# Seven inputs of a Winograd-style convolution loaded as fp32 through nine rotating slots, one casting load left

## The chip, the cores and the metric

The kernel runs on one core of one Trainium2 chip. The metric is the device time of one execution in microseconds (us). A ratio is the mean time of one kernel's fast runs over that of the kernel before in the same rounds, so it is not quite the ratio of the medians quoted beside it.

In the profile PE is TensorE (matmuls), PEld its weight loads, DVE VectorE, ACT ScalarE, POOL GpSimd and SP SyncE, whose queue starts most transfers. A "casting load" is a transfer from HBM that reads fp32 and writes fp16 into SBUF; only GpSimd issues those here, on the software queue q0. All other transfers of the program are on the hardware queue q1; q8 and q14 fetch instructions. A transfer is cut into packets for the 16 DMA engines, and it has landed when all its engines have reported.

## The reference

```python
batch, c_in, h, w, c_out = 16, 64, 64, 64, 128
x_pad = np.pad(x, ((0, 0), (0, 0), (1, 1), (1, 1)), mode='constant')
for b in range(batch):
    for co in range(c_out):
        for ci in range(c_in):
            for kh in range(3):
                for kw in range(3):
                    output[b, co] += weight[co, ci, kh, kw] * x_pad[b, ci, kh:kh+h, kw:kw+w]
```

The input is 16.8 MB of fp32, the output 33.6 MB. Both must cross HBM once.

## The kernel before

Two images form a pair: 64 channels each, 128 partitions together, eight pairs in all. Rows are taken two at a time, so that two output rows share one product `U` of the sum of two input rows (`ss`). TensorE takes fp16, so each fp32 input needs a cast. Pairs 0 to 4 come as fp32 and are cast by ScalarE in quarters; pairs 5 to 7 come through casting loads.

```python
NH = 5
def next_slot(shape, name):                     # 16 KB per partition each
    slot[0] += 1
    return big.tile(shape, F32, tag=f"slot{(slot[0] - 1) % 8}", name=name)

def load(p):                                    # fp32, hardware queue
    xf[p] = next_slot([128, H, W], "xf")
    for lo, hi in cuts if p == 0 else [(0, H)]: # input 0 in four pieces
        keep(nc.sync.dma_start(xf[p][:, lo:hi, :], x_rows[128 * p : 128 * p + 128, lo:hi, :]))

def cast(p, n):
    if p not in xs:
        xs[p] = xpool.tile([128, H, W], F16, tag="xs", name="xs")
    lo, hi = cuts[n]
    keep(nc.scalar.copy(xs[p][:, lo:hi, :], xf[p][:, lo:hi, :]))

def outs(p):
    ots[p] = [next_slot([128, H // 2, 2, W], "ot") for _ in range(2)]

def load_cast(p):                               # fp32 to fp16 on the way
    xs[p] = xpool.tile([128, H, W], F16, tag="xc", name="xc")
    keep(nc.gpsimd.dma_start(xs[p], x_rows[128 * p : 128 * p + 128, :, :]))
# ... weights, sums of pair 0 ...
for p in range(NP):
    # ... GpSimd adds the row pairs of input p + 1; at p == 0 the casting loads are issued
    for blk in range(4):                        # 8 row pairs each
        U = group([(G1, None)])                 # matmuls on ss
        # ScalarE copies U out of PSUM, then runs casts[p][blk]
        A = group([(G21, 1), (G0, -1)])         # VectorE: even rows = A + U
        Bt = group([(G01, 0), (G2, 2)])         # VectorE: odd rows = Bt + U
        # ... after the last block: two stores of 2 MB (the last pair: two halves each)
```

## Time and profile before

| what | before |
|---|---|
| time, median of 4 runs (beside the changed kernel) | 127.97 us |
| span of the profiled run | 126.2 us |
| TensorE busy | 106.4 us, 84% |
| hardware queue q1 / casting loads q0, share of 16 engines | 84.0% / 12.1% |
| ScalarE casts | 20 |

The span is the profiled execution from first to last instruction. "Share of 16 engines" is the time that a queue's packets took, divided by 16 times the span. The lines themselves are in the prediction, with how to read them.

### The profile page before, as it was taken

The numbers are of one execution on the slowest core, as the hardware profiler recorded it, in microseconds if no ns is written. First come the engines' busy times: TensorE is split into PE (matmuls) and PEld (weight loads), VectorE is DVE, ScalarE is ACT, GpSimd is POOL, SyncE is SP. The second block draws the span as 40 slices with busy tenths as digits, with TensorE's granted clock in tenths as the row PEclk, the third lists the DMA queues.
The fourth block names the chain that finished last, engine by engine and source line by source line (L and its number), as shares of the span: only waits on it lengthen the run. The fifth ranks groups of instructions, "written<-read, shape, count | busy, mean of one in ns | idle before, by whom it ended". The sixth has DMA issues, their size and how long they took to land.

```text
span 126.2 us, 2428 instructions
## 1 busy us (share of the span) xinstructions
PE 106.4 (84%) x978; PEld 53.6 (42%) x978; DVE 84.4 (67%) x135; ACT 55.9 (44%) x88; POOL 33.8 (27%) x23
## 2 busy tenths in 40 slices
PE   0479999999999999999999999999999999950000
PEld 0334545554454545454545454455545554520000
DVE  0186777877777777777877787777877787770000
ACT  4183789996969694333333333333333333300000
POOL 2000399959129258004800390000000000000000
PEclk9999999999999999999999999999999999996555
DMA  4999999999999999999999999999999999999970
GB/s 121 298 434 431 426 426 436 343 317 317 288 332 332 312 309 306 369 447 447 410 415 421 436 452 426 415 415 426 452 436 415 421 415 462 423 395 434 423 301 10
DMA packets 4330, 47.62 MB, mean 377 GB/s; under 512 B 480, under 2 KB 480, under 8 KB 1120
## 3 DMA queue, kind: packets, MB, share of 16 engines
q1 hardware_dynamic: 3888, 44.34, 84.0%
q0 software_dynamic: 432, 3.15, 12.1%
q8 instruction: 7, 0.11, 0.3%
q14 instruction: 3, 0.02, 0.0%
HBM read 17.07 MB, written 33.55 MB: 401 GB/s over the span
## 4 chain that ended last, share of the span: by engine, by line
PE 82%; DMA 4%; DVE 2%; issue 1%; DVEq 0%; SPq 0%
PE acc L170 82%; DMA xf<-in_x_dram 4%; DVE ot L190 1%; DVE ss L95 1%; DVE ot L193 0%; DVEq L227 0%; SPq L51 0%; DVEq L190 0%
## 5 line engine op out<-in xcount | busy, mean ns | idle before, releaser
L170 PEld LDWEIGHTS <-Wt 64*128 64x128 f16 x960 | 52.5, 96 | 53.8 <-issue 4.1
L184 ACT COPY ut<-acc 128x512 f32<-128x512 f32 x64 | 34.4, 591 | 49.8 <-issue 45.2
L170 PE MATMUL acc<-xs,Wt 64*128 64x504 f16 (+2 forms) x480 | 56.5, 383 | 0.0
L190 DVE TENSOR_TENSOR ot<-acc,ut 128x512 f32<-128x512 f32 x64 | 41.3, 687 | 22.0 <-PE acc L170 19.6
L193 DVE TENSOR_TENSOR ot<-acc,ut 128x512 f32<-128x512 f32 x64 | 41.2, 685 | 0.6 <-PE acc L170 0.6
L170 PE MATMUL acc<-xc,Wt 64*128 64x504 f16 (+3 forms) x288 | 32.7, 373 | 0.0
L170 PE MATMUL acc<-ss,Wt 64*128 64x504 f16 (+1 forms) x192 | 27.0, 384 | 1.5 <-DVE ss L95 1.5
L95 POOL TENSOR_TENSOR ss<-xf 128x1024 f16<-128x1024 f32 x8 | 18.8, 2378 | 20.0 <-DMA xf<-in_x_dram 15.0
L68 ACT CAST xs<-xf 128x1024 f16<-128x1024 f32 (+2 forms) x20 | 20.4, 1060 | 0.9 <-DMA xf<-in_x_dram 0.9
L95 POOL TENSOR_TENSOR ss<-xc 128x1024 f16<-128x1024 f16 x6 | 12.6, 2125 | 21.0 <-issue 21.0
L113 PE MATMUL wp<-ident,w 128*64 128x128 f16 x18 | 1.3, 328 | 4.2 <-DVE w L85 4.2
L95 DVE TENSOR_TENSOR ss<-xf 128x512 f16<-128x512 f32 x4 | 2.8, 690 | 2.8 <-DMA xf<-in_x_dram 2.8
L85 DVE CAST w<-w_raw 128x576 f16<-128x576 f32 x1 | 0.5, 460 | 3.7 <-DMA w_raw<-in_weight_dram 3.7
L113 PEld LDWEIGHTS <-w 128*64 128x64 f16 x18 | 1.1, 209 | 4.2 <-DVE w L85 4.2
L77 POOL DMA_DIRECT2D xc<-in_x_dram x3 | 1.8, 599 | 0.0
L115 ACT CAST Wt<-wp 128x384 f16<-128x384 f32 x1 | 0.5, 480 | 2.8 <-PE wp L113 2.8
L115 ACT ACT_TABLE_LOAD x1 | 1.3, 1283 | 0.7 <-PEq L216 0.7
L120 ACT CAST Wt<-wp 128x384 f16<-128x384 f32 x1 | 0.5, 481 | 0.5 <-DVE Wt L118 0.5
L117 DVE TENSOR_TENSOR Wt<-wp,Wt 128x384 f16<-128x384 f32 x1 | 0.6, 551 | 0.0
L118 DVE TENSOR_TENSOR Wt<-wp,Wt 128x384 f16<-128x384 f32 x1 | 0.5, 549 | 0.0
L121 ACT CAST Wt<-wp 128x384 f16<-128x384 f32 x1 | 0.5, 487 | 0.0
masks.py:199 POOL TENSOR_SCALAR_AFFINE_SELECT ident<-ident 128x128 f16<-128x128 f16 x1 | 0.3, 293 | 0.1
(5 smaller groups left out, 0.6 us busy)
## 6 DMA issues: line engine op xcount, KB each, us to landing
out_dram<-ot SPq DMA_DIRECT2D x14, 2048.0 KB, 20.4
xf<-in_x_dram SPq DMA_DIRECT2D x4, 2048.0 KB, 19.6
out_dram<-ot SPq DMA_DIRECT2D x4, 1024.0 KB, 11.4
xc<-in_x_dram POOLq DMA_DIRECT2D x3, 1024.0 KB, 24.2
xf<-in_x_dram SPq DMA_DIRECT2D x2, 512.0 KB, 6.2
xf<-in_x_dram SPq DMA_DIRECT2D x1, 576.0 KB, 5.0
xf<-in_x_dram SPq DMA_DIRECT2D x1, 448.0 KB, 7.2
w_raw<-in_weight_dram SPq DMA_DIRECT2D x1, 288.0 KB, 2.9
```

What stands on the lines that cost most here:

```text
L68: keep(nc.scalar.copy(xs[p][:, lo:hi, :], xf[p][:, lo:hi, :]))
L77: keep(nc.gpsimd.dma_start(xs[p], x_rows[128 * p : 128 * p + 128, :, :]))
L85: keep(nc.vector.tensor_copy(w16, w_raw))
L95: eng.tensor_add(ss[p][:, lo : lo + n, :], v[:, lo : lo + n, 0, :], v[:, lo : lo + n, 1, :])
L113: nc.tensor.matmul(wp[q : q + 64, k * CO : k * CO + CO], w16[:, t::9], ident)
L115: keep(nc.scalar.copy(wrow(G1), wps[1]))
L117: keep(nc.vector.tensor_sub(wrow(G21), wps[2], wrow(G1)))
L118: keep(nc.vector.tensor_sub(wrow(G01), wps[0], wrow(G1)))
L170: nc.tensor.matmul(tiles[b2][:, lo - j0 : hi - j0, c_lo:c_hi], Wt[p0 : p0 + 64, wi, kw, :], rhs, start=i == 0, stop=i == n - 1,)
L184: keep(nc.scalar.copy(ut, U[b2]))
L190: nc.vector.tensor_add(ots[p][b2][:, j0 : j0 + RB, 0, :], A[b2], us[b2])
L193: nc.vector.tensor_add(ots[p][b2][:, j0 : j0 + RB, 1, :], Bt[b2], us[b2])
```

## The change

The intent is to take two of the three casting loads off GpSimd's queue. Seven fp32 inputs need more slots (nine) and a deeper ring of fp16 inputs (four). ScalarE, which gets eight more casts, is spared two of them by GpSimd. One buffer of row sums is given up, and the row sums of pairs 3 and 4 are now taken from the fp16 copies. (Changed lines only, without their context.)

```diff
-    xpool = ctx.enter_context(tc.tile_pool(name="xpool", bufs=3))
+    xpool = ctx.enter_context(tc.tile_pool(name="xpool", bufs=1))
-    spool = ctx.enter_context(tc.tile_pool(name="spool", bufs=3))
+    spool = ctx.enter_context(tc.tile_pool(name="spool", bufs=2))
-    NH = 5
+    NH = 7
-        return big.tile(shape, F32, tag=f"slot{(slot[0] - 1) % 8}", name=name)
+        return big.tile(shape, F32, tag=f"slot{(slot[0] - 1) % 9}", name=name)
+    by_pool = [(3, 3), (5, 3)]
-            xs[p] = xpool.tile([128, H, W], F16, tag="xs", name="xs")
+            xs[p] = xpool.tile([128, H, W], F16, tag=f"xs{p % 4}", name="xs")
-        keep(nc.scalar.copy(xs[p][:, lo:hi, :], xf[p][:, lo:hi, :]))
+        copy = nc.gpsimd.tensor_copy if (p, n) in by_pool else nc.scalar.copy
+        keep(copy(xs[p][:, lo:hi, :], xf[p][:, lo:hi, :]))
-    casts[1] = [[(2, 0), (2, 1)], [(2, 2)], [(2, 3), (3, 0)], [(3, 1)]]
-    casts[2] = [[(3, 2), (3, 3)], [(4, 0)], [(4, 1), (4, 2)], [(4, 3)]]
+    casts[1] = [[(2, 0), (2, 1)], [(2, 2), (2, 3)], [(3, 0), (3, 1)], [(3, 2)]]
+    casts[2] = [[(4, 0), (4, 1)], [(4, 2), (4, 3)], [(5, 0), (5, 1)], [(5, 2)]]
+    casts[3] = [[(6, n)] for n in range(4)]
-                sums(nc.gpsimd, p + 1, xf[p + 1] if p + 1 < NH else xs[p + 1], lo, 16)
+                sums(nc.gpsimd, p + 1, xf[p + 1] if p < 2 else xs[p + 1], lo, 16)
+            if p == 1 or p == 2:
+                cast(2 * p + 1, 3)
```

## The prediction

> **What bounds the kernel now.** I began with the page: the busy shares, the row of forty slices and the DMA queues.
>
> ```profile
> PE 106.4 (84%) x978; PEld 53.6 (42%) x978; DVE 84.4 (67%) x135; ACT 55.9 (44%) x88; POOL 33.8 (27%) x23
> ...
> PE   0479999999999999999999999999999999950000
> ...
> DMA  4999999999999999999999999999999999999970
> GB/s 121 298 434 431 426 426 436 343 317 317 288 332 332 312 309 306 369 447 447 410 415 421 436 452 426 415 415 426 452 436 415 421 415 462 423 395 434 423 301 10
> ...
> q1 hardware_dynamic: 3888, 44.34, 84.0%
> q0 software_dynamic: 432, 3.15, 12.1%
> ```
>
> The reader is to see two full rows, not one. TensorE is full from slice 4 to slice 35 and then has nothing to do; the DMA row is full from slice 2 to slice 39, so it begins earlier and ends later. q0 is the three casting loads, q1 all else.
>
> Next the chain of work that ended last, then busy time by stretch.
>
> ```profile
> 1.18 5.03 DMA xf<-in_x_dram
> ...
> 6.97 103.93 PE acc L170 x948
> ...
> 112.85 0.60 DVE ot L193
> ```
>
> The program's own last arithmetic is done at 113.5 us of 126.2. The chain looks like TensorE (82%), but it stops there; the other 12.7 us are the landing of outputs and the end of the program, which it does not attribute. (The last line is a piece of the page's chain in order of time: start, length, what.)
>
> ```profile
> 9.00:21.50 12.50, 12.50 (x106) 6.03 (x104) 8.95 (x15) 9.11 (x14) 6.76 (x6) 1.00 1.02 435
> 21.50:54.50 33.00, 33.00 (x313) 16.67 (x311) 26.08 (x43) 23.45 (x34) 17.95 (x8) 1.00 1.02 330
> 54.50:111.00 56.50, 56.50 (x532) 28.51 (x530) 44.00 (x72) 19.36 (x36) 8.42 (x4) 1.00 1.01 428
> ...
> 114.00:120.00 6.00, 0.00 (x0) 0.00 (x0) 0.00 (x0) 0.00 (x0) 0.00 (x0) 0.54 1.00 423
> 120.00:126.20 6.20, 0.00 (x0) 0.00 (x0) 0.00 (x0) 0.00 (x0) 0.00 (x0) 0.50 0.36 153
> ```
>
> The last two columns are DMA share and GB/s. The share is 1.00 to 1.02 in every stretch from 9 to 120 us. The apparent dip to 330 GB/s in the middle is counting: bytes are those written, and a casting load reads twice what it writes. In those 33 us 330 x 33 = 10.9 MB were written; adding the other half that the casting loads read, 3.15 MB, gives 14.04 MB, or 425 GB/s. So the DMA engines are the bound, TensorE close behind. How close: the last output transfers are issued at 114.5 us (the end of SyncE's row in the timeline). From there 5.5 us x 423 + 6.2 us x 153 = 3.3 MB still move, of which those last transfers are 2.1 MB. The other 1.2 MB are a backlog of 2.8 us. A compute end later by less than that, minus the start delay of a transfer, costs nothing; one earlier gains nothing.
>
> **What the Trainium skill says.** "DMA: Bandwidth & Descriptors", section "Bandwidth", gives 435 GB/s as the ceiling of the ports into SBUF and 425 measured for a 16 MB transfer; the trace agrees, with 435, 425 and 428. The same page, section "SWDGE vs HWDGE vs iDMA", says that a cast during a DMA must be issued from GpSimd, and that software and hardware queues feed the same 16 engines, which take turns between them. The trace agrees: in the casting stretch the two share one total that stays at 425. So taking a load off the one queue and putting it on the other makes no new capacity. "GPSIMD Engine Reference", section 4.1, calls one-input GpSimd work roughly line-rate, and two-input work about half the speed of VectorE. The first page's "Specifications" put the start delay of a hardware-queue transfer at about 0.6 us, which no view here separates; with it the backlog is an estimated 2.2 us. For two inputs on GpSimd this trace has 2.37 us for 1024 columns; a GpSimd cast it does not show.
>
> **The change, part by part.**
>
> *Loads.* Two casting loads leave, two fp32 loads of 2 MB come. In DMA time: q0 has 12.1% for three, that is 4.03% or 5.09 us each; q1 has 84.0% for 44.34 MB, 1.894% per MB, or 3.97% and 5.01 us for a 2.10 MB load. Saved: 2 x 0.08 = 0.16 us. The rates say the same: 425 against 428 over 33 us is 0.23 us for three loads, 0.15 us for two. If pure loading keeps the 435 of the first stretch, two more loads save another 0.16 us. Sum: 0.15 to 0.3 us off the bound. Total bytes from and to HBM do not change.
>
> *Order.* Seven loads now stand ahead of the outputs in the one hardware queue, so the first output (ready at 23.2 us) begins to move at about 45 us instead of 34 to 37. By 45 us 17.07 MB must have been read: 1.2 us start, about 3.3 us lost in the first 6 us, 17.07 MB at 425 = 40.2 us, sum 44.7. The outputs, 33.55 MB at 428, take 78.4 us: 123.1, where the transfers end now too. The queue does not run dry between: pair k's output is ready at about 23 + 12.8k us, and gets its turn at 44.7 + 9.8k; for pair 6 that is 100 against 103.5.
>
> *Slots.* With nine slots, pair 1 writes into the slots of inputs 0 and 1, pair 3 into 4 and 5, pair 4 into input 6 and the first output. That output is sent by about 50 us and its slot is wanted at 74. No slot looks late.
>
> *ScalarE.* Eight casts more, minus two given to GpSimd, against the 20 of now: 26. At 1.06 us (mean of the row of casts) plus 0.59 us per copy, a block with two casts and two copies takes 2.12 + 1.18 = 3.3 us by means; a block on TensorE lasts 12.8 / 4 = 3.2. Copies overlap in the timeline (two take 1.07), so it is 3.2. Pair 0 already has three blocks like this:
>
> ```profile
> 16.75 1.07 ACT L184 COPY ut<-acc 128x512 f32<-128x512 f32 x2 [0.43 <-ACT xs L68]
> 17.71 2.11 ACT L68 CAST xs<-xf 128x1152 f16<-128x1152 f32 x2
> 19.99 1.07 ACT L184 COPY ut<-acc 128x512 f32<-128x512 f32 x2 [0.17 <-ACT xs L68]
> ```
>
> There 0.17 to 0.43 us remain idle, so it just fits, and each fourth block of pairs 1 and 2 has one cast and lets it catch up.
>
> *Arrival.* Inputs 2 and 3 should land as now, input 3 at 27.4 us. Inputs 4, 5 and 6, with one casting load beside them, land at about 35, 40 and 45 us. ScalarE wants them after the copies of pair 2's first block (36.9 us now), of its third (43.3) and of pair 3's first (49.7). The margin is 2 to 5 us.
>
> *GpSimd.* Two casts of 896 columns, which I estimate at 1.2 us each: the two-input add reads 2048 elements in 2.37 us, 1.16 ns each, times 896, and a little. The next sums wait for a free buffer, since there are two instead of three. Pair 3's sums cannot start before TensorE has used those of pair 1, about 32 us, and need 4.2 us, against the 48 us at which they are wanted. This is off the path.
>
> Sum: 127.95 - 0.25 = 127.7 us.
>
> **The rivals.**
>
> *Casting loads are dearer than they look* (descriptor work on GpSimd, stalls). Then two fewer would save more. Against it: their packets' share per byte read is within 2% of the others', and the DMA share never falls below full while they run. The most it could give is the 2.8 us of backlog, where TensorE's end takes over: about 125.3 us.
>
> *A new wait on ScalarE or GpSimd.* If a load comes after ScalarE asks for it, the copies behind it in program order wait, PSUM stays full and TensorE stops. For it: input 4's margin is under 2 us and the blocks are full. Against it: 2.2 to 2.8 us of backlog swallow the first stall. A stall of 3 us would make 128.5 to 130; one at every block with two casts, up to 1 us each over the nine blocks of pairs 0 to 2 that have two casts, 127.7 + 9 - 2 = 135.
>
> *The hidden transfer.* The load's place in time is all that changes, and both queues are behind one full bound: the time stays at 127.9. My main case is this one with the small saving on top.
>
> **Range and chances.** The saving is 0.15 to 0.3 us and the runs before spread 0.3 us. I give 127.0 to 128.6, with a little more room above, for a stall that the backlog does not wholly swallow. Over 2% faster means under 125.4, all that the backlog allows: 0.02. Slower than 130.5 needs a repeated stall: 0.04. Within 2%: 0.94.
>
> **What would show each step.** Right: the DMA row full to slice 38; about 1.05 MB on q0 with some 4% share; 430 GB/s or so in place of 310 to 340 for most of 21 to 54 us; outputs taking 25 us or more to land in the middle; the chain still 104 us of TensorE, its last VectorE add at 113.5 within half a microsecond. Wrong: TensorE below 9 in slices 8 to 16, with casts waiting on the input's DMA; a DMA row with a slice below 9 after slice 20, which would mean that the outputs ran dry; or a last add well after 115 us.

## The result, and the profile after

The changed kernel takes 127.95 us (median of 4 runs, 127.78 to 128.12) beside 127.97 us for the kernel before; the ratio is 1.000, with a 95% interval of 0.998 to 1.0021. Run again later in five rounds (the twelfth run below) it took 127.94 beside 127.91, ratio 0.9994. No change shows. The predicted 127.7 us would be a ratio of 0.998: it lies at the edge of the first interval and inside that of the twelfth run (0.9961 to 1.0027), so the times alone do not exclude a saving of 0.25 us.

From the page of the changed kernel, the DMA row in forty slices, the rate, and the two queues:

```profile
DMA  4999999999999999999999999999999999999960
GB/s 122 304 431 443 427 426 426 348 320 317 393 432 427 429 429 427 421 432 421 437 437 416 442 416 432 437 421 421 432 421 437 437 416 442 413 406 437 429 265 13
...
q1 hardware_dynamic: 4176, 48.53, 91.8%
q0 software_dynamic: 144, 1.05, 4.0%
```

The stretch below 350 GB/s in the middle has shrunk from nine slices to three, because only one casting load is left, but the DMA row above it is as full as it was. The two queues took 96.1% before and take 95.8% now: work went from one to the other.

Busy time by stretch of the changed kernel, at the cuts shown of the kernel before; the last two columns are DMA share and GB/s:

```profile
9.00:21.50 12.50, 12.50 (x108) 6.08 (x106) 9.36 (x15) 9.51 (x14) 5.98 (x4) 1.00 1.01 431
21.50:54.50 33.00, 33.00 (x314) 16.68 (x310) 26.13 (x43) 27.19 (x38) 14.32 (x8) 1.00 1.01 397
54.50:111.00 56.50, 56.50 (x532) 28.44 (x529) 44.00 (x71) 21.11 (x38) 12.62 (x6) 1.00 1.01 428
```

With the 1.05 MB that the casting load reads and does not write, the middle stretch moved 397 x 33 + 1.05 MB = 14.15 MB, or 429 GB/s, against 425 before. The share is full from 9 us on, as before.

Three pieces of the changed kernel's chain of work in order of time (start, length, what):

```profile
1.17 5.13 DMA xf<-in_x_dram
...
7.07 103.52 PE acc L176 x948
...
112.54 0.60 DVE ot L199
```

TensorE's chain is 103.5 us, as before (103.9), and the last arithmetic ends at 113.1 us instead of 113.5. None of it had to wait for the new casts. ScalarE's row of the timeline (start, length, what, idle time before in brackets) in pairs 1 to 3:

```profile
35.65 1.07 ACT L190 COPY ut<-acc 128x512 f32<-128x512 f32 x2 [1.15 <-issue]
36.61 2.11 ACT L71 CAST xs<-xf 128x1152 f16<-128x1152 f32 x2
38.81 1.07 ACT L190 COPY ut<-acc 128x512 f32<-128x512 f32 x2
39.77 1.90 ACT L71 CAST xs<-xf 128x1024 f16<-128x1024 f32 x2
42.05 1.07 ACT L190 COPY ut<-acc 128x512 f32<-128x512 f32 x2 [0.39 <-ACT xs L71]
```

Pair 2's first block starts at 35.65. No ScalarE cast here waits for its input. Three blocks with two casts in a row leave ScalarE 0.4 us idle or less, and the block before had left it 1.15 us. GpSimd's row:

```profile
27.18 0.93 POOL L71 CAST xs<-xf 128x896 f16<-128x896 f32 x1 [1.64 <-DMA xf<-in_x_dram]
32.61 4.21 POOL L98 TENSOR_TENSOR ss<-xs 128x1024 f16<-128x1024 f16 x2 [4.50 <-PE acc L176]
40.50 0.93 POOL L71 CAST xs<-xf 128x896 f16<-128x896 f32 x1 [3.68 <-DMA xf<-in_x_dram]
45.40 4.21 POOL L98 TENSOR_TENSOR ss<-xs 128x1024 f16<-128x1024 f16 x2 [3.97 <-PE acc L176]
```

A GpSimd cast took 0.93 us. The waits of 3.7 to 4.5 us cost nothing: the sums of pair 3, done at 36.8 us, are used from 48 us on.

The two kernels differ in one place that I had not looked at, the end. This is the DMA view of the stretch from 120 to 126 us, forty slices of 0.15 us; first the kernel before, then the changed one:

```profile
DMA  9697979776756556232201001010100000000000
GB/s 601 273 546 328 546 328 546 328 328 273 328 218 273 218 218 273 109 164 109 109 0 55 0 0 55 0 55 0 55 0 0 0 0 0 0 0 0 0 0 0
```

```profile
DMA  3939292919191905010101010101000000000000
GB/s 164 710 164 710 109 601 109 492 55 437 55 437 55 382 0 219 0 55 0 55 0 55 0 55 0 55 0 55 0 0 0 0 0 0 0 0 0 0 0 0
```

A slice with "55" holds one packet of 8 KB, and such a packet comes every second slice: one engine of the sixteen, working alone at 309 ns a packet. By the ends of the packets, the others are done by 122.7 us in the changed kernel and one goes on to 124.5; in the kernel before the others end by 123.3, and the last one ends at 124.5 too. In this stretch 0.95 MB moved before and 0.75 MB after, so the engines on average are ahead by 0.2 MB, or 0.47 us at 428 GB/s (the median engine by 0.41 us). The program ends with the last engine, and that one gained nothing; what holds it up is told under run 4.

### The profile page after: what moved, and what is told of

Same layout as the page of the kernel before. It is cut to its first block, busy times and chain, and to the rows that moved or that the text cites. A ratio compares the mean times of both kernels' runs of the same rounds, so it can differ in the third digit from the quotient of the medians.

```text
span 126.0 us, 2439 instructions
## 1 busy us (share of the span) xinstructions
PE 106.0 (84%) x978; PEld 53.4 (42%) x978; DVE 84.4 (67%) x135; ACT 61.7 (49%) x94; POOL 33.6 (27%) x23
## 3 DMA queue, kind: packets, MB, share of 16 engines
q0 software_dynamic: 144, 1.05, 4.0%
## 4 chain that ended last, share of the span: by engine, by line
PE 82%; DMA 4%; DVE 2%; issue 1%; DVEq 0%; SPq 0%
PE acc L176 82%; DMA xf<-in_x_dram 4%; DVE ot L196 1%; DVE ss L98 1%; DVE ot L199 0%; DVEq L233 0%; SPq L51 0%; DVEq L196 0%
## 5 line engine op out<-in xcount | busy, mean ns | idle before, releaser
L176 PE MATMUL acc<-xs,Wt 64*128 64x504 f16 (+3 forms) x672 | 77.9, 379 | 0.0
L71 ACT CAST xs<-xf 128x1024 f16<-128x1024 f32 (+2 forms) x26 | 26.7, 1066 | 1.0 <-DMA xf<-in_x_dram 1.0
L98 POOL TENSOR_TENSOR ss<-xs 128x1024 f16<-128x1024 f16 x8 | 16.8, 2124 | 25.7 <-PE acc L176 25.7
L98 POOL TENSOR_TENSOR ss<-xf 128x1024 f16<-128x1024 f32 x4 | 9.4, 2370 | 14.2 <-DMA xf<-in_x_dram 14.2
L176 PE MATMUL acc<-xc,Wt 64*128 64x504 f16 (+3 forms) x96 | 10.9, 373 | 0.0
L98 POOL TENSOR_TENSOR ss<-xc 128x1024 f16<-128x1024 f16 x2 | 4.2, 2131 | 8.6 <-issue 8.6
L71 POOL CAST xs<-xf 128x896 f16<-128x896 f32 x2 | 1.9, 929 | 5.3 <-DMA xf<-in_x_dram 5.3
L118 ACT CAST Wt<-wp 128x384 f16<-128x384 f32 x1 | 0.5, 479 | 2.8 <-PE wp L116 2.8
L123 ACT CAST Wt<-wp 128x384 f16<-128x384 f32 x1 | 0.5, 478 | 0.5 <-DVE Wt L121 0.5
L80 POOL DMA_DIRECT2D xc<-in_x_dram x1 | 0.7, 694 | 0.0
## 6 DMA issues: line engine op xcount, KB each, us to landing
xc<-in_x_dram POOLq DMA_DIRECT2D x1, 1024.0 KB, 15.4
```

The costliest lines, as they stand in the source:

```text
L71: keep(copy(xs[p][:, lo:hi, :], xf[p][:, lo:hi, :]))
L98: eng.tensor_add(ss[p][:, lo : lo + n, :], v[:, lo : lo + n, 0, :], v[:, lo : lo + n, 1, :])
L118: keep(nc.scalar.copy(wrow(G1), wps[1]))
L176: nc.tensor.matmul(tiles[b2][:, lo - j0 : hi - j0, c_lo:c_hi], Wt[p0 : p0 + 64, wi, kw, :], rhs, start=i == 0, stop=i == n - 1,)
```

## The experiments

The theory to test: the transfers set the time, TensorE close behind; a casting load costs the DMA engines almost what an fp32 load does; and the end is set by the one engine that is last. All runs but the three load studies are edits of the changed kernel, unless said otherwise.

### Runs 1 and 2: TensorE held up

```diff
+ if p == 1 and blk == 0 and i == 0 and wi == G1 and b2 == 0:
+     for _ in range(10):            # run 2: 24
+         for h in (0, 64):
+             nc.tensor.matmul(tiles[h // 64][:, 0:RB, :], Wt[h : h + 64, wi, kw, :],
+                              ss[p][h : h + 64, lo:hi, :], start=True, stop=True)
```

> The changed kernel with TensorE held up once, early in pair 1, by ten extra pairs of matmuls whose result is overwritten; by the two halves running side by side that is 10 x 0.213 = 2.1 us (estimate from 480 pairs of matmuls in the 103.5 us of the chain, 0.216 us a pair). Theory (the transfers set the end, with 2.2 to 2.8 us of backlog when the last outputs are issued): last VectorE add about 2.1 us later than 113.1 us, time within 0.5 us of 127.95. Rival (TensorE's chain sets the end): 127.95 + 2.1 = 130.1 us.

> The same with 24 extra pairs, 5.1 to 5.2 us. Theory: the backlog of 2.2 to 2.8 us is used up and the rest shows: 127.95 + 5.1 - 2.5 = about 130.6 us, with a dip of the DMA share below full near the end. Rival (TensorE's chain): 133.1 us. Rival (a backlog much larger than I counted): under 129 us.

Run 1 took 128.47 us beside 127.90 (ratio 1.005, 1.0024 to 1.0075); its extra matmuls took 2.16 us. Run 2 took 130.55 us (ratio 1.0208, 1.0168 to 1.0247); its extra matmuls took 5.18 us. Of 2.16 us about 0.5 show, of 5.18 about 2.6. TensorE's chain alone does not set the end. The four times of run 2 fall into two groups (129.8 and 130.0, 131.2 and 131.3 us), so its loss is 2.0 or 3.3 us by the group; its trace is of the slowest. But the place of the loss is not where I had put it. Busy time by stretch, run 1:

```profile
99.00:102.00 3.00, 3.00 (x32) 1.54 (x30) 2.27 (x5) 0.91 (x3) 0.00 (x0) 1.00 0.88 371
102.00:105.00 3.00, 3.00 (x32) 1.56 (x30) 2.42 (x5) 1.06 (x2) 0.00 (x0) 1.00 0.92 388
```

and run 2:

```profile
102.00:106.00 4.00, 4.00 (x41) 2.09 (x39) 3.27 (x6) 1.67 (x4) 0.00 (x0) 1.00 0.36 147
106.00:120.00 14.00, 11.49 (x108) 5.72 (x104) 10.09 (x17) 3.70 (x7) 0.00 (x0) 1.00 0.99 417
```

The transfers run dry at 99 to 106 us, while TensorE works on: the stores of pair 6 have not come yet. From 106 us to the end they are full again. The missing share in run 1 is 3 x 0.12 + 3 x 0.08 = 0.6 us, about the 0.57 us lost by the medians (the profiled execution itself lost 0.8).

### Run 9: the same hold, pair 6's stores in halves

```diff
-            parts = {3: (0, 64)} if p < NP - 1 else {1: (0, 32), 3: (32, 64)}
+            parts = {3: (0, 64)} if p < NP - 2 else {1: (0, 32), 3: (32, 64)}
```

> TensorE held up by 2.16 us as in the first run, but pair 6's stores also cut in halves, so that the first half can go 6.4 us before its last block. In the first run the DMA row dipped to 7 and 310 GB/s at slice 33 (about 103 us), where pair 6's stores had not come yet. Theory (the 0.5 us lost there are that gap): the dip goes and the time is back within 0.25 us of 127.95. Rival (it is the last pair's own stores that are late): 128.4 again.

The ten extra pairs of matmuls of run 1 are in it too. It took 128.03 us beside 127.88, ratio 1.0005 (0.9988 to 1.0021), with TensorE just as late as in run 1. The same stretches:

```profile
99.00:102.00 3.00, 3.00 (x32) 1.55 (x29) 2.27 (x5) 1.07 (x2) 0.00 (x0) 1.00 1.01 423
102.00:105.00 3.00, 3.00 (x32) 1.54 (x28) 2.42 (x5) 1.07 (x2) 0.00 (x0) 1.00 0.95 401
```

The gap is mostly gone, and the loss with it. So, in this kernel, 2 us of TensorE are worth nothing when the stores are there in time, and the transfers are the bound.

### Run 5: fewer bytes

```diff
-            if blk in parts:
+            if blk in parts and p != 3:
```

> The changed kernel without the two stores of pair 3 (4.2 MB of 50.6 MB; the result is wrong on purpose). All arithmetic stays. Theory (transfers bound, TensorE close behind): 4.2 MB are 9.8 us of transfer at 428 GB/s, but the end can come forward only to where TensorE holds it: last stores issued at 113.2 us, 2.1 MB or 4.9 us of transfer, about 2 us for start and landing, so the last landing at about 120.1 instead of 124.5, and the time near 123.5 us. The lone late engine should also have nothing to be late with, since all engines wait for data before the last stores. Rival (TensorE's chain alone sets the end): 127.95, unchanged. Rival (transfers alone, TensorE far off): 118.2 us.

Without 4.2 MB the kernel takes 124.63 us beside 127.87 (ratio 0.9739, 0.9711 to 0.9767). That is 3.2 us of the 9.8 us that those bytes take, as the theory has it: transfers are the bound, and TensorE is 3 us behind. The time is 1.1 us above my number. Busy time by stretch:

```profile
78.00:100.00 22.00, 22.00 (x210) 11.11 (x206) 17.44 (x28) 7.06 (x15) 4.21 (x2) 1.00 0.73 311
...
114.00:120.00 6.00, 0.00 (x0) 0.00 (x0) 0.00 (x0) 0.00 (x0) 0.00 (x0) 0.74 0.98 415
120.00:122.00 2.00, 0.00 (x0) 0.00 (x0) 0.00 (x0) 0.00 (x0) 0.00 (x0) 0.50 0.04 16
```

The transfers are idle for a quarter of the time from 78 to 100 us, and are full again at the end. A late engine is still there in the last line, with the last landing at about 121 us. The records of the last store's landings put it 0.9 us after the median engine. That part of the expectation was wrong: engines that had just waited together were apart again 15 us later.

### Runs 6 to 8: loads by themselves

```python
for n in range(24):
    t = big.tile([128, H, W], F32, tag=f"slot{n % 8}", name="xf")      # run 8: F16
    keep(nc.sync.dma_start(t, x_rows[...]))                             # runs 7, 8: nc.gpsimd
```

> Loads by themselves: 24 fp32 loads of 2 MB on the hardware queue (each pair three times), then one 2 MB store; no convolution, the result is wrong on purpose. By 5.01 us a load: 24 x 5.01 = 120 us by share, or at 431 to 435 GB/s 116 to 117 us, plus 3 us of start and 7 us for the closing store: 127 us. It is the yardstick for the next two runs.

> The same 24 fp32 loads issued by GpSimd on the software queue, without a cast. Tells the cost of the queue from that of the cast. My theory (no cost in either beyond 2 percent): within 1 us of the run before it. Rival (descriptors written by GpSimd cost): 2 us or more longer.

> The same 24 loads as casting loads. The prediction's working (5.09 against 5.01 us each): 24 x 0.08 = 1.9 us longer than on the hardware queue. Rival one (casting loads really cost the same, so the 0.15 us was never there): within 0.5 us. Rival two (they are much dearer): 5 us or more.

The times were 130.02, 131.03 and 130.56 us, in the same rounds. Busy time by stretch, one line each of runs 6, 7 and 8 (busy columns: VectorE and GpSimd):

```profile
6.00:118.00 112.00, 0.00 (x0) 0.00 (x0) 1.00 1.01 429
```

```profile
6.00:118.00 112.00, 0.00 (x0) 8.44 (x16) 1.00 1.01 429
```

```profile
6.00:118.00 112.00, 0.00 (x0) 8.44 (x16) 1.00 1.03 215
```

Read bytes move at 429, 429 and 2 x 215 = 430 GB/s. A casting load costs the engines the same as an fp32 load. What differs is the start: in the first six microseconds run 6 has 254 GB/s, run 7 186. The casting run was 0.54 us longer than run 6, or 0.02 us a load in place of the 0.08 that I had taken from the queue shares, and it was shorter than the fp32 loads on the same queue. Rival one was nearest, by its number just missed (0.54 against 0.5 us), as run 7 just missed its 1 us (1.01). Run 6 missed its 127 us by 3: its last packet did end at 127.0, and the sum had left out what follows. These runs also show no late engine: run 6's landings of each of 24 loads lie between 0.50 us before and 0.30 us after the median engine, from the first load to the last, and its page has no row of instruction fetches (q8). The convolution has seven fetches in q8, and one engine at its end is 1.8 us behind the next; run 4 was to test whether the one causes the other.

### Run 3: one store over fifteen engines

```diff
+ cs = [(0, 120), (120, 128)] if (p, blk, b2) == (NP - 1, 1, 0) else [(0, 128)]
+ for c0, c1 in cs:
      keep(nc.sync.dma_start(out_rows[2 * p + b2, c0:c1, lo:hi, :], ...[c0:c1, lo:hi, :]))
```

> The changed kernel with one 1 MB store of the last pair (first half, first image) cut into partitions 0 to 119 and 120 to 127. By the Trainium skill (DMA: Bandwidth & Descriptors, section on why a DMA increments its semaphore by 16) 120 partitions go over the 15 lowest-numbered engines and 8 over the lowest 8, so the highest-numbered engine is spared 8 packets of 8 KB, 8 x 0.306 = 2.4 us. Theory (one DMA engine of the 16 drains alone at the end, in single packets from about 122.9 to 124.5 us, and sets the time), if it is the highest-numbered one: the lone tail goes, the time falls by 1.0 to 1.6 us, to about 126.5. If the lone engine is another one: the tail stays, 127.9 to 128.3. Rival (all engines end together, the mean rate sets the time): no change, since the bytes are the same.

It took 130.32 us beside 127.90, ratio 1.0213 (1.0173 to 1.0254), worse than either theory had. Busy time by stretch, run 3 first, then the unedited changed kernel:

```profile
112.00:117.00 5.00, 0.29 (x4) 0.00 (x0) 1.65 (x3) 0.00 (x0) 0.00 (x0) 0.77 0.98 338
```

```profile
112.00:117.00 5.00, 0.00 (x0) 0.00 (x0) 1.14 (x2) 0.00 (x0) 0.00 (x0) 1.00 0.98 416
```

The engines are busy, but the store moves bytes more slowly, and the last engine is done at 127 us. The page's count of small packets rose by 7, which is 15 + 8 - 16, so the store was spread over 15 and 8 engines as expected. Why such a store is slow is left open. It says nothing on which engine is the late one, since the slower store hides it.

### Run 4: more instruction fetches

```diff
+            if 3 <= p <= 6:
+                for _ in range(192):
+                    keep(nc.gpsimd.memset(scrap, 0.0))
```

> The changed kernel with 768 one-element GpSimd memsets, 192 in each of pairs 3 to 6, where GpSimd idles. Theory (the lone engine is late because it alone carries the instruction fetches, 7 of 16 KB in the page's q8 row): the q8 row grows from 7 to about 10 fetches, and if they use the same engine its tail gets about 3 x 0.6 = 1.8 us longer and the time rises by 1 to 1.8 us, to 129 to 129.7. Rival (that engine is slow for another reason, or other engines' fetches go elsewhere): q8 grows, the time stays within 0.3 us of 127.95.

It took 184.27 us. A failed experiment: a one-element memset occupies GpSimd for 156 ns, so that 192 of them no longer fit where it idles, and the sums behind them came late. From its timeline:

```profile
49.21 29.93 POOL L146 MEMSET scrap<- 128x1 f32 x192
79.13 4.17 POOL L99 TENSOR_TENSOR ss<-xs 128x1024 f16<-128x1024 f16 x2
```

The q8 row stayed at 7 fetches; the row q14 rose from 3 to 9. So q8 does not carry GpSimd's instructions. In runs 1 and 2, where TensorE has 40 and 96 instructions more, q8 has 8. Whether the fetches make the late engine late was not settled by this run.

The packet records of the traces, which no view prints, do settle it. They name no engine, but a packet starts within a few ns of the end of the one before it on its engine, so a row of packets can be followed. Between 45.2 and 112.2 us of the changed kernel there is one unbroken row of 104 packets of 16 KB that took 633 to 672 ns each (mean 648), while 1607 of the other 1622 such packets of the hardware queue took 611: one engine, slower by 3.8 us in sum. In the kernel before this row has 90 packets, from 54.3 to 112.3 us, and 3.4 us in sum. In both it is the last of the sixteen to land the 13th store of 2 MB (109.6 and 109.7 us), and followed on it can end with the packet that ends the program; in runs 1 and 5 no other end is possible. The five fetches of q8 in that time do not interrupt the row: the packets lengthened to 0.91 to 1.02 us belong to other rows. So the late engine is late because its packets of stores are slow, and not because of the fetches. In run 6 no load packet between 5 and 120 us took more than 639 ns, and there is no such row. Why one engine is slower while the stores run is not known.

This also suggests why the gain went missing. With the loads done at 45 us instead of 54, the slow row begins earlier and has 14 packets more, 0.47 us of extra, about what the other engines gained. Runs 10 and 11, the same two kernels with two further edits, show the same (92 and 79 packets, 3.36 and 2.90 us). It is argued from these traces; no run tested it.

### Runs 10 to 12: an attempt at a faster one, and controls

Run 10 is the changed kernel with pair 6's stores in halves (the edit of run 9) and this one. Run 11 is the kernel before with both edits. Run 12 is the changed kernel unaltered.

```diff
-        for lo, hi in cuts if p == 0 else [(0, H)]:
+        for lo, hi in [(0, 18), (18, H)] if p == 0 else [(0, H)]:
```

> An attempt at a faster one: pair 6's stores in halves, and input 0 loaded in two pieces (rows 0 to 18 and 18 to 64) instead of four. The last three pieces are 1.5 MB and took about 3.8 us (landings 6.4 to 10.3 us), 394 GB/s against 431 for whole loads. Theory (transfers bound, also at the start): 0.3 us earlier, 127.6, ratio 0.997. Rival (second block waits for its rows, TensorE later by up to 1 us; or the gain is lost on the lone engine): 127.9 to 128.3.

> The kernel before with the same two edits as the tenth run (input 0 in two pieces, pair 6's stores in halves), three casting loads kept. If the gain of the tenth run (127.71, ratio 0.9981) belongs to these edits, it is the same here: 127.7, ratio 0.998. If the fp32 loads of the change are needed for it (the saving I had predicted, 0.15 to 0.3 us, comes to light only with them), it stays at 127.9, ratio 1.000.

> The changed kernel once more, unaltered, for a tighter ratio beside the same runs of the kernel before. Theory (no saving is left at the end): ratio 1.000 within 0.0015. The prediction's own number (127.7 against 127.95): 0.998.

Run 10 took 127.71 us beside 127.88, ratio 0.9981 (0.9965 to 0.9997). Run 11 took 127.81 beside 127.91, ratio 0.9984 (0.9956 to 1.0012), run 12 127.94, ratio 0.9994 (0.9961 to 1.0027). The two edits are worth about 0.2 us; the interval of run 10 just excludes none. Run 11 has the same within its wider interval, so the gain does not show a need for the fp32 loads. Run 10 is the fastest kernel, by an amount without practical weight. In the stretch after 120 us it moved 0.69 MB, run 11 0.81 and run 12 0.75; all three end with one engine alone until 124.4 to 124.7 us. Run 12's interval includes both 1.000 and the predicted 0.998, so it did not decide between them (one run of the kernel before took 129.08 us in those rounds and widens it).

## Why the prediction was right or wrong

**The bound: right.** Transfers were named as the bound, with TensorE close behind. Run 5 shows both sides of it: bytes taken away shorten the time, by 3.2 us and no more. Run 9 shows that 2.16 us of TensorE can be hidden once pair 6's stores go in halves. The reading that the chain of waits stops short of the end, and that the DMA share decides, held.

**The saving of 0.25 us: not seen, and its terms were too large.** The step that failed is "Sum: 127.95 - 0.25 = 127.7 us". Measured were 0.02 us by the medians (the intervals reach to 0.26 us in the first comparison and 0.5 in the twelfth run). Its first term, 0.08 us per load from the two queues' shares, measured 0.02 by itself (runs 6 and 8), and that came from the start and not from the rate. Its second term, 435 GB/s for pure loads, measured 431 in the changed kernel's first stretch and 429 in run 6. The middle stretch did gain 4 GB/s, and the median engine ended some 0.4 us earlier, in one trace of the kernel before and two of the changed one. But the end is the last engine's, and that did not move (124.5 us before, 124.5 and 124.7 after). The prediction had reckoned with the mean of 16 engines, where one engine with packets of 648 instead of 611 ns sets the end.

**The order of transfers: right.** The last fp32 input had landed by 45.2 us (issued at 7.6, longest time to landing 37.6), against the 44.7 of the working, and the queue did not run dry after it.

**ScalarE and arrivals: right.** The blocks with two casts fit, with up to 0.4 us idle. Input 3 came at 27.2 us (27.4 predicted) and input 5 at 40.5 (40). Input 4 was there when ScalarE asked for it at 36.6. The wait that would have taken the place of the one removed did not appear.

**GpSimd: right.** Its cast took 0.93 us instead of the estimated 1.2, off the path. Pair 3's sums began at 32.6 us (about 32).

**The backlog: wrong in place, and its size agreed by luck.** I had worked out 2.2 to 2.8 us at the last stores. Run 2 hid 5.18 - 2.6 = 2.6 us (1.9 to 3.2 by its two groups). But that is the slack of another place: the transfers ran dry at pair 6's stores, where I had compared 100 us with 103.5 and thought no more of it; run 1 lost 0.5 us there with a delay of 2.16 us. In that comparison I had left out the start of a store and its issue. Of the slack at the last stores the runs show only that 2.16 us fit in it (run 9).

**The rivals.** Dear casting loads are refuted by runs 6 to 8. A new wait did not come. The hidden transfer, "the time stays at 127.9", is what happened; the right case was named, and a small saving was put on top that did not arrive.

## What to carry to other kernels

Here every DMA engine was full almost from start to end, and moving loads between queues changed nothing that could be measured; fewer bytes did (run 5), and so did an idle moment filled (run 9). Do not count half-size written bytes of casting loads as a dip, and look at the last microseconds slice by slice: the mean of the engines can get better while the last engine, which ends the program, does not. For slack against a full queue, check every hand-over and not only the last: here the tightest was the pair before the last, whose stores came in one piece.

## What the Trainium skill lacked or had wrong

- "DMA: Bandwidth & Descriptors": it gives no cost for a cast during a transfer. Here 24 loads of 2 MB moved at 429 GB/s as fp32 on either queue, and at 430 read as casting loads.
- The same page, on the spread of a transfer by its number of partitions: it gives the 15 engines for 120 partitions, and the packet count agrees, but not that such a store is slow. The stretch with it moved 338 GB/s against 416.
- The same page, start delays of about 1 us on the software and 0.6 on the hardware queue: from the start of the first issuing instruction to the first packet it was 1.37 us in run 7 and 1.00 us in run 6. The difference of 0.4 agrees; both delays are longer. (Run 7's 24 loads ended 1.09 us later than run 6's, 121.94 against 120.85 us, also because its first issue came 0.51 us later.)
- The same page, "Latency and other measured facts", calls engines 7 and 15 usually slower than the rest, gives no amount, and guesses at the rings of the software queue as the cause. Here one engine's 16 KB packets took 648 ns instead of 611 and it ended 1.8 us after the next. The slow row began at 45.2 us, 10 us after the last transfer of the software queue had landed (issued at 19.5, 15.4 us to landing), so rings in use at the time do not explain it here. The records name no engine, so whether it is one of those two is open.
- "GPSIMD Engine Reference", section 4.1: one-input work at about line rate agrees with 0.93 us for a cast of 896 columns (ScalarE's shortest casts took 0.95). The page gives no price for tiny instructions: 192 one-element memsets took 29.9 us, 156 ns each.
